# Layer one's narrow gate blocks as a pair of seven products, between two parts of the value pair

## The chip, the cores and the metric

The kernel runs on one core of one Trainium2 chip. The time is that of the device, in microseconds; the figure to be predicted is the median of several runs. A core has five engines that run their own instruction streams and meet at semaphores: TensorE (PE, matmuls; its weight loads are shown as PEld), VectorE (DVE), ScalarE (ACT), GpSimd (POOL) and SyncE (SP, which here issues most of the loads). DMA engines move data between the chip's memory and the on-chip buffers.

## The reference

A trunk of two layers over 512 tokens of 2048 features, in float32. Each layer normalises its input, projects it by one matrix whose columns serve two groups of heads and their gates, runs gated linear attention on one group and chunked attention on the other, and projects the result back:

```python
h = rmsnorm(x, g_pre)
z = h @ w_in
gq, gk, gv, gg, ga, aq, ak, av, ag = split_columns(z)
log_a = jax.nn.log_sigmoid((ga @ w_alpha + b_alpha).astype(jnp.float32)) / GLA_TAU
o_gla = gla_chunk_causal(...)
o_att = chunk_band_attention(...)
...
o_att = o_att * jax.nn.silu(ag)
y = jnp.concatenate([o_gla, o_att], axis=-1) @ w_out
return x + rmsnorm(y, g_post)
```

The change touches the columns `av` (values of the chunked attention, 1024 columns), `ag` (its gate, 1024) and `ga` (the 16 columns from which the forget gate is made). `ag` and `ga` are held as one block of 512 columns (AG0) and two narrow ones of 264 (AG1, AG2), the 16 of `ga` at the end of AG2.

## The kernel before, in words

**Products.** Each float32 operand is split into a high and a low part in PE's own format, and a product is the sum of three matmuls: high by high, high by low, low by high. The 2048 features are 8 chunks of 256; tokens are 4 groups of 128. Weights come as tiles of 128 x 1024 (two feature groups of 512 columns; 128 x 528 for a narrow block): a load by SP, a cast on ACT to the high part (`wh`, L240), a subtraction on DVE to the low part (`wl`, L250).

**Standard blocks and pairs.** `std_gemm` (L341) multiplies all tokens by one block: 8 chunk jobs of 24 matmuls. `fast_gemm` (L372) takes two blocks at once, as a 2 x 2 product of halves (tokens in two halves, features in two halves, two column blocks) with seven half-size products, P1 to P7, instead of eight. Each product has 4 chunk jobs (c0 to c3) of 12 matmuls. The price lies beside PE: sums and differences of weight tiles (L234, L236) and of token operands, and combinations of the accumulators at the end. The token sums are S1 to S4, the left operands of P5, P6, P3 and P7; P4's is A22, the second half of tokens and features. They are made in `make_sums` (L609), split, and written to memory by GpSimd; a later load brings them to a ring of four buffers, `sa`, which jobs use in turn.

**Order.** A list, `stream`, holds every job in the order in which PE takes them. `ahead()` (L295) prepares the jobs that follow: loads up to five jobs ahead, high parts four, low parts three. DVE work that does not belong to jobs (normalisation, sums, gates) is a list of `tasks`, advanced by `rate` steps a job; within an engine, instructions run in the order in which they were issued. Buffers in the ring and the named slots (`g0` to `g17`) can be taken again only when their last reader is done.

**The start of layer 0.** The wide block AG0 runs on raw tokens, since the normalisation is not known yet. Meanwhile `first_operands` (L706) normalises and splits the tokens, half after half within each chunk. Then the narrow blocks AG1 and AG2 run as standard blocks, while DVE makes the token sums. Then the value pair (AV0, AV1) runs all seven products in the order PROD; only S1 stays on the chip, the other sums are loaded. Then come the first query-key pair and the rest.

**Layer 1** already runs the narrow blocks as a pair (order PROD_GATE), and the value pair in two parts around half of AG0 (PROD_FRONT, PROD_REST).

Of the kernel before, what the change touches and what calls it, by code (L numbers as in the profile page):

```python
# [15 lines left out]
P = 128  # L16
# [20 lines left out]
def hybrid_trunk(  # L37
# [105 lines left out]
    PROD_REST = order("50 51 52 53 60 61 30 62 63 31 70 32 71 72 73 33 40 41 42 43")  # L143
    PROD_GATE = order("10 50 11 51 12 52 13 53 60 30 61 31 62 32 63 33 70 71 72 73 20 40 21 41 22 42 23 43")
# [6 lines left out]
    class Job:  # L151
        def __init__(self, l, kind, c, b0, b1=None, pair=None):
            self.l, self.kind, self.c, self.b0, self.b1, self.pair = l, kind, c, b0, b1, pair
            self.a = None
            self.parted = l == L - 1 and kind != "std" and b0 == AV0
# [19 lines left out]
        def load(self):  # L175
# [10 lines left out]
            elif k == "P1":  # L186
                h = slot(f"g{4 + c}", [2, 512]) if self.parted else rtile("H")
                p["H", self.c] = self.fetch(h, b0, top)
                last_h[0] = last_load[0]
            elif k == "P5" and self.parted:  # L190
# [3 lines left out]
            elif k == "P5":  # L194
                p["r", self.c] = self.fetch(rtile("raw", bufs=5), b1, top)
# [10 lines left out]
            else:  # L206
                home = k == "P5" and b0 == AV0
# [7 lines left out]
            elif src is not None and b0 != NB_IN and not home:  # L215
                until(lambda: k == "P4" or (id(sums), LEFT[k], c) in written)
# [7 lines left out]
        def high(self):  # L224
# [3 lines left out]
            else:  # L228
# [3 lines left out]
                with tc.issue_after(lows[-4 if early else -2]) if self.b0 >= NB_IN else nullcontext():  # L232
                    if k == "P6" or (k == "P5" and not self.parted) or (k == "P4" and (self.b0 >= NB_IN or self.parted)):
# [25 lines left out]
    for l in range(L):  # L259
        if l:  # L260
            pr = {}
            stream += [Job(l, "std", c, AG0) for c in CO]
            stream += [Job(l, k, c, *PAIRS[0], pr) for k, c in PROD_FRONT]
            stream += [Job(l, "std", c, AG0) for c in CO]
            stream += [Job(l, k, c, *PAIRS[0], pr) for k, c in PROD_REST]
            qk = {}
            pr = {"next": qk}
            stream += [Job(l, k, c, *GATE_PAIR, pr) for k, c in PROD_GATE]
        else:
            stream += [Job(l, "std", c, b) for b in (AG0, AG1, AG2) for c in CO]  # L270
        for b0, b1 in PAIRS[1:] if l else PAIRS:
            pr = qk if l and b0 == QK01 else {}
            stream += [Job(l, k, c, b0, b1, pr) for k, c in PROD]
# [28 lines left out]
    written = set()  # L302

# [36 lines left out]
    def std_gemm(l, blk, outs, chunks, operand, evac, rate=0.0, skip=0, lag=0):  # L340
        wide = W if blk == AG0 else N1  # L341
        pss = {o: ps_mm.tile([P, W], F32, tag="mm", name=nm("mm"))[:, :wide] for o in outs}
# [29 lines left out]
    def fast_gemm(l, pair, consume, rate=0.0, skip=0, feature_major=False, after=None, end=False, lag=0, ops=A, prod=None, acc=None):  # L372
        b0 = pair[0]
        gates = b0 == AG1
        wide = N1 if gates else W
        parted = acc is not None
        if not parted:
# [6 lines left out]
        if parted:  # L384
            target.update(P5="Z", P3="Z")
        if prod is None:
# [17 lines left out]
        def finished(k, t):  # L404
# [8 lines left out]
            elif k == "P2":  # L413
                consume(0, 0, t, None, combine(acc[target[k]][t], keep["p1"][t], ALU.add, keep["p1"][t]))
            elif k == "P4":
# [35 lines left out]
        for k, c in prod:  # L451
            if k == "P2" and (end or gates) and c == 0 or k == "P5" and parted and c == 0:
# [11 lines left out]
            with tc.issue_after(half_turns[1]) if (k, c) == ("P4", 3) and half_turns else nullcontext():  # L464
                matmuls(job, k, c, range(2))
            ahead()
# [44 lines left out]
    STAGE = ("g6", "g7", "g4", "g5", "g10")  # L511
    HOME = {("S1", c): tag for c, tag in enumerate(("g9", "g14", "g15", "g2"))}
    HOMES = {**HOME, **{("S2", c): tag for c, tag in enumerate(("g12", "g13", "g8", "g11"))}}
# [94 lines left out]
    def make_sums(dst, tags, parts, home={}):  # L608
        stage = [0]  # L609

        def sub(out, a, b):
            nc.vector.tensor_tensor(out=out, in0=a, in1=b, op=ALU.subtract)
# [13 lines left out]
        for c in range(4):  # L626
            a11, a12, a21, a22 = parts(c)
            yield
            sub(a22, a21, a22)
            put("S1", c, a22)  # L630
            yield
# [963 lines left out]
```

## Time and profile before

| what | value |
|---|---|
| median of 3 runs | 1590.28 us (1589.94 to 1592.12) |
| the profiled execution | 1594.45 us |
| its span in the profile | 1592.7 us |
| mean granted clock of PE | 0.999 |
| DMA | 441.45 MB, mean 277 GB/s |
| memory written | 61.62 MB |

The profile is of one execution, which took 1594.45 us; its span, from the first to the last instruction, is 1592.7. The costliest groups of instructions are matmuls of `fast_gemm` (L445; L435 where features are the rows of the result), then the casts and subtractions that split weights:

```profile
L445 PE MATMUL mm<-wh,sa 128*128 128x512 f32 (+1 forms) x1600 | 501.1, 387 | 1.8 <-DMA sa<-S 1.3
L240 ACT CAST wh<-H 128x1024 fp32r<-128x1024 f32 (+1 forms) x240 | 245.2, 1024 | 191.9 <-PE mm L445 78.9
L250 DVE TENSOR_TENSOR wl<-H,wh 128x1024 fp32r<-128x1024 f32 (+1 forms) x240 | 284.0, 1186 | 72.2 <-PE mm L445 25.4
```

Columns: line, engine, operation, output and inputs by the program's names, shapes and count; then the busy time in us and the mean of one in ns; then the idle time of the engine just before them, and what ended most of it. The mean of a matmul is longer than the time from one to the next, since matmuls overlap.

### The profile page before, as it was taken

The page shows a single profiled execution, that of the slowest core. Times are in us where ns is not written, and L with a number is a line of the kernel's source. Part 1 is how long each engine was busy: PE and PEld are TensorE (multiplying, and loading weights), DVE is VectorE, ACT ScalarE, POOL GpSimd, SP SyncE. Part 2 cuts the span into 40 slices and gives each one's busy share as a digit, 9 for nine tenths or more (in the row PEclk, how much of TensorE's full clock was granted, in tenths as well). Part 3 has the DMA queues.
Part 4 walks back from the last instruction along what each step waited for, and adds up shares of the span by engine and source line. Part 5 has one row for each costly group of instructions (what it writes and reads, how often), then busy time and mean ns, then how long its engine had stood idle before and what let it go on. Part 6 is the DMA issues. An engine that isn't in the chain of part 4 may idle for free.

```text
span 1592.7 us, 25038 instructions
## 1 busy us (share of the span) xinstructions
PE 1578.6 (99%) x9102; PEld 1369.3 (86%) x9102; DVE 1277.0 (80%) x1697; ACT 920.0 (58%) x1535; POOL 130.8 (8%) x222
## 2 busy tenths in 40 slices
PE   9999999999999999999999999999999999999998
PEld 7998999998888777888888899999988887778886
DVE  5978768678687878998989878775886878699887
ACT  7554445557465556664786456455574645476644
POOL 0220000000000000100122000000010000001001
PEclk9999999999999999999999999999999999999999
DMA  9698686685867869689889998847868597686887
GB/s 355 229 407 310 224 278 231 215 294 196 301 201 273 283 209 330 219 305 398 301 262 356 382 332 311 285 153 261 298 224 300 174 312 256 228 319 230 339 304 201
DMA packets 137739, 441.45 MB, mean 277 GB/s; under 512 B 15364, under 2 KB 27908, under 8 KB 137584
## 3 DMA queue, kind: packets, MB, share of 16 engines
q1 hardware_dynamic: 119952, 377.86, 67.5%
q0 software_dynamic: 17376, 61.70, 11.0%
q8 instruction: 72, 1.18, 0.3%
q14 instruction: 51, 0.42, 0.1%
q10 hardware_dynamic: 288, 0.30, 0.1%
HBM read 380.23 MB, written 61.62 MB: 277 GB/s over the span
## 4 chain that ended last, share of the span: by engine, by line
PE 86%; DVE 5%; DMA 5%; issue 2%; ACT 1%; SPq 0%; POOLq 0%; DVEq 0%; ACTq 0%
PE mm L445 51%; PE mm L435 17%; PE mm L358 6%; DMA raw<-in_w_dram 4%; PE ax L445 4%; DVE wl L250 2%; PE ax L1015 2%; PE ax L998 1%; PE ax L1204 1%; PE ax L1174 1%; PE ax L978 1%; PE ax L976 1%; PE ax L977 1%; ACT wh L240 1%; PE ax L1296 0%
## 5 line engine op out<-in xcount | busy, mean ns | idle before, releaser
L445 PE MATMUL mm<-wh,sa 128*128 128x512 f32 (+1 forms) x1600 | 501.1, 387 | 1.8 <-DMA sa<-S 1.3
L240 ACT CAST wh<-H 128x1024 fp32r<-128x1024 f32 (+1 forms) x240 | 245.2, 1024 | 191.9 <-PE mm L445 78.9
L445 PEld LDWEIGHTS mm<-wh,sa 128*128 128x128 f32 x1600 | 297.7, 188 | 64.9 <-ACT wh L240 3.0
L240 ACT CAST wh<-raw 128x1024 fp32r<-128x1024 f32 (+2 forms) x237 | 235.9, 1002 | 197.9 <-PE mm L445 87.4
L250 DVE TENSOR_TENSOR wl<-H,wh 128x1024 fp32r<-128x1024 f32 (+1 forms) x240 | 284.0, 1186 | 72.2 <-PE mm L445 25.4
L250 DVE TENSOR_TENSOR wl<-raw,wh 128x1024 fp32r<-128x1024 f32 (+2 forms) x237 | 272.5, 1154 | 49.3 <-PE mm L435 17.8
L445 PE MATMUL mm<-wl,sa 128*128 128x512 f32 (+1 forms) x800 | 310.1, 388 | 0.6 <-DVE wl L250 0.5
L435 PE MATMUL mm<-sa,wh 128*128 128x256 f32 x1280 | 237.8, 285 | 0.0
L445 PE MATMUL mm<-wh,a 128*128 128x512 f32 (+1 forms) x672 | 215.5, 387 | 0.0
L435 PEld LDWEIGHTS mm<-sa,wh 128*128 128x128 f32 x1280 | 200.3, 191 | 0.6
L435 PE MATMUL mm<-sa,wl 128*128 128x256 f32 x640 | 181.1, 284 | 0.5 <-DVE wl L250 0.5
L445 PEld LDWEIGHTS mm<-wl,sa 128*128 128x128 f32 x800 | 150.2, 188 | 31.9 <-DVE wl L250 2.3
L234 DVE TENSOR_TENSOR H<-H,raw 128x1024 f32<-128x1024 f32 (+1 forms) x136 | 160.8, 1185 | 1.6 <-DMA raw<-in_w_dram 1.0
L445 PEld LDWEIGHTS mm<-wh,a 128*128 128x128 f32 x672 | 125.2, 188 | 24.6
L445 PE MATMUL mm<-wl,a 128*128 128x512 f32 (+1 forms) x336 | 130.6, 389 | 0.5 <-DVE wl L250 0.5
L435 PEld LDWEIGHTS mm<-sa,wl 128*128 128x128 f32 x640 | 122.3, 191 | 0.9 <-DVE wl L250 0.9
L445 PE MATMUL mm<-wh,g 128*128 128x512 f32 (+1 forms) x416 | 120.4, 366 | 0.0
L236 DVE TENSOR_TENSOR raw<-H,raw 128x1024 f32<-128x1024 f32 (+1 forms) x52 | 61.5, 1182 | 48.4 <-DMA raw<-in_w_dram 48.3
L435 PE MATMUL mm<-a,wh 128*128 128x256 f32 x512 | 94.8, 285 | 0.0
L489 POOL TENSOR_TENSOR sm<-sm,mhalf 128x2 f32<-128x2 f32 (+2 forms) x40 | 38.0, 951 | 690.8 <-DVE sm L1025 367.1
L395 ACT COPY ev<-mm 128x512 f32<-128x512 f32 (+1 forms) x112 | 64.1, 573 | 52.8 <-PE mm L445 37.6
L445 PEld LDWEIGHTS mm<-wh,g 128*128 128x128 f32 x416 | 75.3, 188 | 13.4 <-ACT ev L395 0.6
(276 smaller groups left out, 2428.2 us busy)
## 6 DMA issues: line engine op xcount, KB each, us to landing
raw<-in_w_dram SPq DMA_DIRECT2D x287, 512.0 KB, 5.2
sa<-S SPq DMA_DIRECT2D x188, 512.0 KB, 4.7
H<-in_w_dram SPq DMA_DIRECT2D x56, 512.0 KB, 5.1
sa<-A SPq DMA_DIRECT2D x48, 512.0 KB, 6.3
sa<-oS SPq DMA_DIRECT2D x32, 512.0 KB, 5.7
S<-g POOLq DMA_DIRECT2D x30, 512.0 KB, 8.1
raw<-in_w_ag_dram SPq DMA_DIRECT2D x32, 264.0 KB, 4.3
oS<-g POOLq DMA_DIRECT2D x16, 512.0 KB, 4.8
```

Of the source, the lines that this page charges most:

```text
L234: nc.vector.tensor_tensor(out=h, in0=h, in1=r, op=ALU.add)
L236: nc.vector.tensor_tensor(out=r, in0=h, in1=r, op=ALU.subtract)
L240: last_cast[0] = nc.scalar.copy(self.wh[:, z, :], src[:, z, :]).ins
L250: last_low[0] = nc.vector.tensor_tensor(out=self.wl[:, z, :], in0=self.src[:, z, :], in1=self.wh[:, z, :].bitcast(F32), op=ALU.subtract).ins
L358: nc.tensor.matmul(pss[o], a(part, kk, o) if callable(a) else a[:, part, t], rhs[:, kk, :], start=(i == 0 and kk == 0 and m == 0), stop=(i ...
L395: last_copy[0] = nc.scalar.copy(e, src[t]).ins
L435: nc.tensor.matmul(dst, lhs[:, kk, f], a[:, part, tok], start=(fresh and kk == 0 and m == 0 and ft % 2 == 0), stop=(c == 3 and kk == 1 and ...
L445: last_mm[0] = nc.tensor.matmul(out_ps[t], a[:, part, tok], rhs[:, kk, :], start=(fresh and kk == 0 and m == 0), stop=(c == 3 and kk == 1 ...
L489: nc.gpsimd.tensor_tensor(out=out_r, in0=v, in1=mhalf[:, : v.shape[-1]], op=ALU.pow)
L976: nc.tensor.matmul(ps[:, :n], self.qh[:, t], self.kh[:, :n], start=True, stop=False)
L977: nc.tensor.matmul(ps[:, :n], self.qh[:, t], self.kl[:, :n], start=False, stop=False)
L1015: nc.tensor.matmul(o, self.pt[i][:, j * P : (j + 1) * P], av[hd // 4, j // 2][:, j % 2, (hd % 4) * P : (hd % 4 + 1) * P], start=(j == 0), ...
```

## The change

In layer 0 the narrow blocks become a pair of seven products, and the order of work becomes: AG0 whole; P2 and P1 of the value pair; P2 and P1 of the narrow pair; P5, P6, P3, P7, P4 of the value pair; the same five of the narrow pair. The accumulators of the narrow pair's first products stay in the auxiliary PSUM buffers in the meantime. The tokens are normalised by halves: the first half of all chunks, then the second. The sums are made name by name (S1, S2, S4, S3) instead of chunk by chunk, S3 after P3 has been issued; they stay on the chip for the value pair, which therefore loads only A22. For the narrow pair S4, S3, A22 and the last chunk of S1 are loaded. P5's weight sum in the value pair is made by an accumulating DMA of GpSimd onto the tile of P1, no longer by DVE; the narrow pair's P1 tile is loaded a second time for P5. The first operands of the first query-key pair are loaded into slots early, as layer 1 does already. Layer 1's own orders are as they were.

The core of the diff:

```diff
+    PROD_LATE = order("50 51 52 53 60 61 62 63 30 31 32 33 70 71 72 73 40 41 42 43")
+    PROD_LATE_GATE = order("50 51 52 53 60 61 62 63 30 31 70 32 71 33 72 73 40 41 42 43")
...
-            self.parted = l == L - 1 and kind != "std" and b0 == AV0
+            self.parted = kind != "std" and (b0 == AV0 or (b0 == AG1 and l == 0))
+            self.summed = self.parted and b0 == AV0
...
-                h = slot(f"g{4 + c}", [2, 512]) if self.parted else rtile("H")
+                h = slot(f"g{4 + c}", [2, 512]) if self.summed else rtile("raw", bufs=5) if self.parted else rtile("H")
...
             elif k == "P5":
+                if self.parted:
+                    p["H", self.c] = self.fetch(rtile("H"), b0, top)
                 p["r", self.c] = self.fetch(rtile("raw", bufs=5), b1, top)
...
-                home = k == "P5" and b0 == AV0
+                home = b0 == AV0 and k != "P4" or b0 == AG1 and (k == "P6" or (k == "P5" and c < 3))
...
+        pr, qk = {}, {}
+        pg = {"next": qk}
+        stream += [Job(l, "std", c, AG0) for c in CO]
+        stream += [Job(l, k, c, *PAIRS[0], pr) for k, c in PROD_FRONT]
         if l:
...
         else:
-            stream += [Job(l, "std", c, b) for b in (AG0, AG1, AG2) for c in CO]
+            stream += [Job(l, k, c, *GATE_PAIR, pg) for k, c in PROD_FRONT]
+            stream += [Job(l, k, c, *PAIRS[0], pr) for k, c in PROD_LATE]
+            stream += [Job(l, k, c, *GATE_PAIR, pg) for k, c in PROD_LATE_GATE]
...
+            elif l == 0:
+                op = A[name, c] = rtile("sa", (2, 512), F32R)
...
+            for name in ("S1", "S2", "S4", "S3"):
+                for c in range(4):
+                    while name == "S3" and (0, AV0, "P3", c) not in issued:
+                        yield
+                    make(name, c)
+                    yield
...
-        for ch in CO:
-            kh, c = divmod(ch, 4)
-            while ch not in U:
-                yield
-            for half in range(2):
+        for half in range(2):
+            for ch in CO:
+                kh, c = divmod(ch, 4)
+                while ch not in U:
+                    yield
...
+                if half and kh == 0:
+                    ends.append(made.ins)
+                    yield
+                    continue
...
-            tasks.append(token_sums(l))
-            std_gemm(l, AG1, range(NT), CO, operand_in, gate_evac(1), rate=1.0, lag=1)
-            std_gemm(l, AG2, range(NT), CO, operand_in, gate_evac(2), rate=1.0, lag=2)
-            drain()
...
-            fast_gemm(l, PAIRS[0], av_consume, rate=0.5)
+            std_gemm(l, AG0, range(NT), CO, operand_raw, raw_evac, rate=0.25, lag=1)
+            acc = {n: [ps_mm.tile([P, W], F32, tag="mm", name=nm("mm")) for _ in range(2)] for n in "YX"}
+            fast_gemm(l, PAIRS[0], av_consume, rate=2, prod=PROD_FRONT, acc=acc)
+            acc_g = {n: [aux()[:, :N1] for _ in range(2)] for n in "YX"}
+            tasks.append(token_sums(l))
+            fast_gemm(l, GATE_PAIR, gate_consume, rate=1, prod=PROD_FRONT, acc=acc_g)
+            acc["Z"] = [ps_mm.tile([P, W], F32, tag="mm", name=nm("mm")) for _ in range(2)]
+            fast_gemm(l, PAIRS[0], av_consume, rate=1, prod=PROD_LATE, acc=acc)
+            drain()
+            fast_gemm(l, GATE_PAIR, gate_consume, prod=PROD_LATE_GATE, acc=acc_g)
```

Counted over the whole program: PE has 720 matmuls of 264 columns before and 672 after, with all others alike; DVE goes from 1697 to 1727 instructions, ACT gains 12 casts of 528 columns and 8 copies of 264 among others, SP's DMAs go from 777 to 790 and POOL's from 158 to 162.

Two places of the instruction order. The first is DVE where the value pair's second weight sums begin. Before, the weight lows (`wl`) and the weight sums of P6 (into `H`) of the value pair stand almost alone:

```order
L250 TENSOR_TENSOR wl_199_1287<-H_190_1184,wh_192_1212 128x1024
L250 TENSOR_TENSOR wl_200_1289<-H_187_1154,wh_198_1285 128x1024
L234 TENSOR_TENSOR H_190_1184<-H_190_1184,raw_203_1295 128x1024
L800 COPY g16_195_1231<-mm_173_1025 128x16 x3
L250 TENSOR_TENSOR wl_209_1320<-H_201_1291,wh_202_1293 128x1024
L250 TENSOR_TENSOR wl_212_1339<-H_190_1184,wh_210_1323 128x1024
L234 TENSOR_TENSOR H_201_1291<-H_201_1291,raw_214_1343 128x1024
```

In the changed kernel the same engine, where the value pair goes from P5 to P6 (`g4` to `g6` hold the weight tiles; L630 makes a token sum and L110 its low part; `wl_191_1067` is the low part for P6, chunk 0):

```order
L630 TENSOR_TENSOR H_89_512<-H_89_512,g2_127_718 128x512
L241 TENSOR_TENSOR g4_107_632<-g4_107_632,raw_181_1014 128x1024
L110 TENSOR_TENSOR g8_178_994<-g2_127_718,g8_178_994 128x512
L257 TENSOR_TENSOR wl_187_1043<-g7_126_716,wh_180_1012 128x1024
L241 TENSOR_TENSOR g5_116_662<-g5_116_662,raw_189_1048 128x1024
L630 TENSOR_TENSOR H_100_589<-H_100_589,g3_134_749 128x512
L110 TENSOR_TENSOR g11_184_1025<-g3_134_749,g11_184_1025 128x512
L241 TENSOR_TENSOR g6_121_689<-g6_121_689,raw_193_1072 128x1024
L243 TENSOR_TENSOR raw_212_1193<-g4_107_632,raw_212_1193 128x1024
L257 TENSOR_TENSOR wl_191_1067<-g4_107_632,wh_188_1046 128x1024
```

Token sums and their lows now stand between the weight work, ahead of P6's first low part; before, they were done in the narrow blocks.

The second place is SP, where the operand A22 of the value pair's P4 is loaded (`A2200` is chunk 0 in memory). Before, sums and weight tiles take turns:

```order
L172 DMA raw_274_1660<-in_w_dram 128x1024
L219 DMA sa_264_1602<-S302_92 128x1024
L172 DMA raw_281_1701<-in_w_dram 128x1024
L219 DMA sa_268_1623<-S303_93 128x1024
L172 DMA raw_288_1741<-in_w_dram 128x1024
L219 DMA sa_277_1679<-A2200_98 128x1024
L172 DMA raw_303_1832<-in_w_dram 128x1024
L219 DMA sa_284_1719<-A2201_99 128x1024
```

In the changed kernel at the same operand (`g14`, `g15`, `g2` are the first operands of the next pair, `in_w_ag` is the narrow blocks' weights):

```order
L175 DMA raw_225_1264<-in_w_dram 128x1024
L175 DMA raw_229_1288<-in_w_dram 128x1024
L175 DMA g14_286_1562<-in_w_dram 128x1024
L175 DMA raw_235_1317<-in_w_dram 128x1024
L175 DMA g15_292_1586<-in_w_dram 128x1024
L175 DMA raw_239_1338<-in_w_dram 128x1024
L175 DMA raw_243_1359<-in_w_dram 128x1024
L175 DMA g2_300_1627<-in_w_dram 128x1024
L226 DMA sa_231_1295<-A2200_98 128x1024
L167 DMA raw_248_1382<-in_w_ag_dram 128x528
L167 DMA raw_256_1412<-in_w_ag_dram 128x528
L226 DMA sa_236_1319<-A2201_99 128x1024
```

The loads of S3 are gone; three tiles of the next pair stand in front of A22 instead, and the weight tiles follow one another without an operand between.

More of the change, by code (lines that the diff above doesn't have):

```diff
@@ L215, in load @@
             elif src is not None and b0 != NB_IN and not home:
+                if self.summed and not self.l:
+                    until(lambda: ("S3", 3) in A)
                 until(lambda: k == "P4" or (id(sums), LEFT[k], c) in written)
@@ L302, in hybrid_trunk @@
     written = set()
+    issued = set()
     def pump(n):
@@ L340, in std_gemm @@
     def std_gemm(l, blk, outs, chunks, operand, evac, rate=0.0, skip=0, lag=0):
-        wide = W if blk == AG0 else N1
-        pss = {o: ps_mm.tile([P, W], F32, tag="mm", name=nm("mm"))[:, :wide] for o in outs}
+        pss = {o: ps_mm.tile([P, W], F32, tag="mm", name=nm("mm")) for o in outs}
         pace = Pace(rate, skip)
@@ L373, in fast_gemm @@
         b0 = pair[0]
-        gates = b0 == AG1
-        wide = N1 if gates else W
         parted = acc is not None
+        apart4 = parted and not l
+        gates = b0 == AG1 and not parted
+        wide = N1 if b0 == AG1 else W
         if not parted:
@@ L385, in fast_gemm @@
             target.update(P5="Z", P3="Z")
+        if apart4:
+            target.update(P4="Z")
+            starts.append("P4")
         if prod is None:
@@ L451, in fast_gemm @@
         for k, c in prod:
-            if k == "P2" and (end or gates) and c == 0 or k == "P5" and parted and c == 0:
+            if k == "P2" and (end or gates) and c == 0 or k == "P5" and parted and c == 0 and "Z" not in acc:
                 acc["Z"] = [aux()[:, :wide], aux()[:, :wide]]
@@ L731, in first_operands @@
                 ends.append(split(op[:, 0, :], op[:, 1, :], dst))
-                if half and kh:
+                if half:
                     nc.gpsimd.dma_start(sa_d[0]["A22", c], flat(op))
@@ L735, in first_operands @@
                 yield
-        yield from load_forget_gate(0)
     warm = t2((S,), BF16)
@@ L763, in load_forget_gate @@
     def load_forget_gate(l):
-        raw = slot("g10" if l else "g12", [2, 512])
+        raw = slot("g10", [2, 512])
         fac = slot("g13", [2, 512], F32R)
@@ L894, in raw_evac @@
             gate(0, o, ps, r0[:, o : o + 1])
[L896 to L903 removed]
         av = {}
[L906 removed]
+        AVT = {1: ("g0", "g1"), 0: ("g17", "g3")}
         def av_consume(j, h, t, src, comb):
             if (j, h) not in av:
[L910 removed]
+                if not l:
+                    until(lambda: all((1, 1, c) in A for c in range(4)))
+                av[j, h] = slot(AVT[j][h], [2, 512])
             dst = av[j, h][:, t, :]
```

90 lines of the change are left out of this document (44 added, 46 removed).

## The prediction

> **What bounds the kernel now.** The page's busy shares come first, then the chain that ended last.
>
> ```profile
> PE 1578.6 (99%) x9102; PEld 1369.3 (86%) x9102; DVE 1277.0 (80%) x1697; ACT 920.0 (58%) x1535; POOL 130.8 (8%) x222
> PE 86%; DVE 5%; DMA 5%; issue 2%; ACT 1%; SPq 0%; POOLq 0%; DVEq 0%; ACTq 0%
> ```
>
> TensorE (PE) is the bound, but 99% flatters it: matmul ends are modelled, so a short wait can hide in "busy". I therefore count matmuls. Two rows of the chain in layer 1, where twelve matmuls of one product and chunk run together, give the pitch:
>
> ```profile
> 883.40 2.72 PE mm L445 x12
> 954.01 1.44 PE mm L445 x12
> ```
>
> These are 2.72 / 12 = 0.227 us for a matmul of 512 columns and 1.44 / 12 = 0.120 us for one of 264. Next I cut the start of layer 0 into stretches (columns after the span's length: PE, PEld, DVE, ACT, POOL busy with instructions; then granted clock, DMA share, GB/s):
>
> ```profile
> 36.00:56.00 20.00, 20.00 (x110) 17.43 (x109) 20.00 (x40) 12.54 (x21) 3.66 (x7) 1.00 0.54 181
> 56.00:76.00 20.00, 19.03 (x150) 18.15 (x149) 19.98 (x38) 12.56 (x24) 3.69 (x8) 1.00 0.80 262
> 76.00:100.00 24.00, 24.00 (x197) 23.83 (x196) 20.73 (x39) 12.96 (x23) 9.75 (x19) 1.00 1.02 388
> 100.00:174.00 74.00, 74.00 (x329) 61.07 (x328) 56.04 (x55) 33.38 (x37) 1.67 (x3) 1.00 0.90 335
> ```
>
> The clock is full throughout. From 36 to 76 us VectorE (DVE) is busy without a gap; from 56 to 76 only 150 narrow matmuls ran, 150 x 0.120 = 18.0 us of work in 20: **2.0 us were lost**. The chain names the engine:
>
> ```profile
> 34.63 21.42 PE mm L358 x114
> 56.05 0.62 DVE wl L250
> 56.67 0.60 DVE g L612
> 58.40 0.88 DVE H L719 x2
> 59.29 0.60 DVE g L110
> ...
> 75.15 24.79 PE mm L358 x200
> ```
>
> Weight lows (L250), gate work (L612), first normalisation (L719) and operand lows (L110) were taken one after another on DVE, and PE waited. After 76 us PE runs unbroken. So layer 0's narrow blocks start DVE-bound and end PE-bound.
>
> **The change part by part.**
>
> 1. *Fewer matmuls.* The two narrow blocks go from 384 matmuls to 7 x 4 x 12 = 336, all of 264 columns; no other count changes. 48 x 0.120 = **-5.8 us**, if PE stays the bound.
>
> 2. *The old DVE stall goes* with the blocks that had it: after the wide block PE now has value products of 2.72 us a chunk, each needing one weight low, where a narrow one lasted 24 x 0.120 = 2.88 us and needed a low and an operand. **-2.0 us** (0 to -2.0).
>
> 3. *What is late next.* DVE's work isn't gone: the sums for the value pair must now be made before its late products begin. In the changed order the place is P6, chunk 0, of the value pair. For the DVE durations:
>
> ```profile
> 36.38 0.87 DVE L719 SCALAR_TENSOR_TENSOR H<-g,gcol,bias 128x256 f32<-128x256 f32 x2
> 37.17 0.87 DVE L719 SCALAR_TENSOR_TENSOR g<-g,gcol,bias 128x256 f32<-128x256 f32 x2
> 37.96 2.73 DVE L119 SCALAR_TENSOR_TENSOR g<-g,gcol,sa 128x512 fp32r<-128x512 f32 x4
> 40.61 0.68 DVE L110 TENSOR_TENSOR a<-H,a 128x512 fp32r<-128x512 f32 x1
> ...
> 107.84 1.22 DVE L234 TENSOR_TENSOR H<-H,raw 128x1024 f32<-128x1024 f32 x1
> 108.97 0.68 DVE L815 COPY g<-ax 96x512 f32<-96x512 f32 x1
> ```
>
> From start to start: 0.79 us for a pair of L719, so 0.40 each; 2.65 for four of L119; 1.13 for 1024 columns. From the first normalisation to the low of P6 c0, the changed order has 38 operations of 512 columns (20 operand or sum lows, 16 sums, 2 gate steps) at 0.60 = 22.8; 8 narrow lows at 0.62 = 5.0; 18 of 1024 columns (14 lows, 4 weight sums) at 1.13 to 1.14 = 20.4; 32 normalisation halves at 0.40 = 12.8; 4 of L119 = 2.65; and 2 combinations of 264 columns, which no row shows, about 0.35 each by half the 0.62 of 528. In all 64.35 us without a gap, begun at 36.38 as now (nothing ahead of it moves): the low ends at 100.7. PE's side:
>
> ```profile
> 50.80 0.28 PE L358 MATMUL mm<-wh,a 128*128 128x264 f32 x1
> ```
>
> The wide block ends at 50.80. Then 8 value jobs, 8 narrow jobs and P5's 4 value jobs: 8 x 2.72 + 8 x 1.44 + 4 x 2.72 = 44.2, so P6 c0 can start at 95.0; its first two matmuls need only the high half, 0.45 more. 100.7 - 95.4 = 5.3 of waiting, and 0.2 at the next chunk: **+5.5 us**. Start-to-start durations hold to about 1.5%, which is 1 us in 64: 4.5 to 6.5. I take the middle. It is a difference of two long sums, and so the term I trust least.
>
> 4. *The A22 operand of P4, chunk 0* (value pair). Its load takes the ring buffer that P7 c0 sets free; P4 c0 starts 3 products later, 3 x 2.72 = 8.2 us. The lead is the same now, and nothing waits, as these rows show:
>
> ```profile
> L219 SPq DMA_DIRECT2D sa<-A x48: 319/382/1386, 146.8 to 1406.7; - x48
> DMA to landing us min/median/max: 3.3/6.5/11.3
> ```
>
> In the changed order nine SP loads (six weight tiles of products and three first operands of the next pair, taken ahead of time) stand between the tile of P7 c0 and this operand, and three POOL stores beside them: 12 x 0.524 = 6.3 MB within the 13.6 us of five products. That is 463 GB/s asked. What the engines gave when full, between 85 and 120 us:
>
> ```profile
> DMA packets 4077, 14.34 MB, mean 410 GB/s; under 512 B 524, under 2 KB 524, under 8 KB 4072
> q1 hardware_dynamic: 2247, 7.97, 56.0%
> q0 software_dynamic: 1825, 6.31, 46.0%
> raw<-in_w_dram SPq DMA_DIRECT2D x9, 512.0 KB, 13.9
> ```
>
> So a backlog forms: 6.3 MB at 410 GB/s take 15.3 us, 1.7 over. The landing lies between 6.5 (median of this operand) and 13.9 us (a load of the same size in the full stretch): a wait between 0 and 13.9 - 8.2 = 5.7. Neither end is nearer: demand is above what they gave, as in the full stretch, but for a short time only. I take 10.5: **+2.3 us**.
>
> [...]
>
> 5. *The rest of the narrow pair* is 20 jobs of 12 matmuls, 28.8 us. DVE's share: 16 weight sums or differences and 20 lows at 0.62, and 8 combinations at 0.35 to 0.7: 25 to 28 us. It is nearly a second bound. Layer 1 runs such a pair today:
>
> ```profile
> 924.00:948.00 24.00, 24.00 (x192) 23.62 (x191) 18.23 (x28) 13.51 (x26) 0.00 (x0) 1.00 0.86 297
> ```
>
> 192 x 0.120 = 23.0 in 24: 1.0 lost. For 28.8 us that is **+1.2 us** (0.3, if DVE's work spreads evenly, to 2.4, twice the row, as DVE is fuller here).
>
> 6. *The first query-key pair* finds its first four operands loaded. It loses today:
>
> ```profile
> 220.00:232.00 12.00, 11.49 (x94) 11.17 (x94) 7.59 (x8) 4.03 (x4) 0.00 (x0) 1.00 0.73 257
> 212.58 5.42 DMA raw<-in_w_dram
> 220.49 6.50 DMA raw<-in_w_dram
> ```
>
> 0.5 idle, and the chain goes through its loads: **-0.3 us** (0 to -0.9).
>
> 7. *Costed at nothing.* Twelve more casts of 528 columns and eight copies on ScalarE (ACT): ACT is busy 12.96 of 24 us and 33.38 of 74. Uncovered they would be 20 x about 0.5 = 10 us, but they lie over 120 us of PE work. Four weight loads of P5 become accumulating DMAs of POOL, which the order issues over 20 us ahead of P5:
>
> ```profile
> g<-in_w_dram POOLq DMA_DIRECT2D x4, 512.0 KB, 7.6
> ```
>
> 7.6 us to landing in layer 1, so they are hidden; if the lead went, each would cost up to 7.6 - 2.72 = 4.9. The new wait of S3's four sums for P3 keeps those sums behind P3's operands on DVE; behind them stand the lows of P7 and P4, two products ahead of PE. DVE is busy 56.04 of 74 there, so I cost it at nothing; without that slack it would be S3's own 12 operations, 7.2 us, spread over P3 and P7.
>
> **Sum:** -5.8 - 2.0 + 5.5 + 2.3 + 1.2 - 0.3 = **+0.9 us**. The profiled execution took 1594.45 (span 1592.7); with the change 1595.35 (span 1593.6). It lies 4.2 above the median of the runs, 1590.28, so the forecast for the median is **1591.2 us**. The matmuls saved are eaten by a DVE wait that has moved and grown, and by a load that comes late.
>
> **The rivals.**
>
> *A, slower: the DMA backlog decides.* Term 4 at its upper end: A22 lands 13.9 us after its issue, 5.7 late, and the total is 0.9 - 2.3 + 5.7 = +4.3, **1594.6 us**. The place is the wait ahead of P4 c0 of the value pair, the point 8.2 us from issue to landing. For it: 463 GB/s asked where 410 was the most seen, and POOL's stores in the same engines. Against it: the engines are 0.90 busy, not full, over the 74 us of the present value pair, and the DVE wait of term 3 gives the loads 5.5 us to catch up.
>
> *B, faster: DVE keeps up.* If the 64 us of DVE work come out 3.5 shorter (the normalisation halves at 0.29, say) and A22 is in time: -5.8 - 2.0 + 2.0 + 0 + 1.2 - 0.3 = -4.9, **1585.4 us**. For it: many of these operations had waits of others between them in the row I took them from. Against it: DVE shows 20.00 and 19.98 busy of 20 in two stretches with this very mix.
>
> *C: the change doesn't do what it says.* The late narrow pair is DVE-bound from end to end, so 48 fewer matmuls buy nothing there: term 5 at 2.4 and one more microsecond for the four combinations that fall together at P7: +3.1, **1593.4 us**. For it: 28 of 28.8 us. Against it: layer 1's row, DVE 18.23 of 24.
>
> **How the numbers follow.** Forecast 0.60, A 0.20, B 0.13, C 0.07. The forecast's own range is -2 to +3, from term 3 (1 either way) and term 4 (2.3 down). For 8 in 10 it must reach into A and most of the way to B: **1586.5 to 1595.8**. About 0.2%, 3.2 us, is what a measurement of this kernel can tell from no change: below 1587.1 lies B with little else, 0.14; above 1593.5 lie A and the upper part of C, 0.23; between them 0.63.
>
> **What would show it.** Right: the first narrow stretch (after the wide block) shows no PE idle; one wait of 4.5 to 6.5 us on DVE (a weight low) about 95 us, at the start of P6; then one of 1 to 4 us on a DMA of an A22 operand about 130 to 140; 336 narrow matmuls in layer 0; from the query-key pair on, the same times with a constant offset. Term 3 is wrong if DVE has gaps between 40 and 95 us or PE's wait there is under 3; term 4 if the operand lands within 8.2; term 5 if the last 240 narrow matmuls take under 29.1 or over 31.2 us. The whole is wrong if layer 1 shifts against layer 0, which nothing in the instruction order suggests.

## The result

The layer that the title calls one is layer 0 of the code. The changed kernel takes 1604.09 us (median; 1603.16 to 1604.71), the kernel before 1590.47 in the same series (1589.94 to 1592.12): 13.6 us slower, a ratio of 1.0083 with a 95% interval of 1.0066 to 1.0101. The forecast was 1591.2 with a range of 1586.5 to 1595.8, so it is wrong: a time above 1593.5 had been given a chance of 0.23, and even the upper rival, 1594.6, is 9.5 us short.

The page of the changed kernel (busy shares, and the chain that ended last by engine):

```profile
PE 1575.7 (98%) x9054; PEld 1365.9 (85%) x9054; DVE 1291.4 (81%) x1727; ACT 927.2 (58%) x1551; POOL 135.4 (8%) x226
PE 86%; issue 4%; DMA 4%; DVE 3%; ACT 1%; POOL 1%; SPq 0%; POOLq 0%; DVEq 0%; ACTq 0%
```

48 matmuls are gone, and the span is 1601.9 us instead of 1592.7. The stretches of layer 0's start (columns as before, granted clock after the busy times):

```profile
36.00:56.00 20.00, 19.15 (x85) 15.50 (x84) 20.00 (x40) 14.24 (x21) 2.42 (x4) 1.00 0.80 293
56.00:76.00 20.00, 20.00 (x99) 16.96 (x98) 19.79 (x31) 9.69 (x16) 5.74 (x8) 1.00 0.87 214
76.00:100.00 24.00, 20.22 (x118) 18.24 (x118) 20.68 (x30) 13.08 (x22) 4.83 (x9) 0.93 0.92 361
100.00:140.00 40.00, 35.54 (x154) 28.27 (x152) 34.44 (x36) 21.01 (x27) 4.79 (x9) 1.00 0.79 285
140.00:174.00 34.00, 31.19 (x196) 28.36 (x197) 23.38 (x35) 12.63 (x23) 0.78 (x2) 0.95 0.94 338
```

The old loss between 56 and 76 us is gone. In its place PE idles 3.8 us in the third row, 4.5 in the fourth and 2.8 in the fifth, and the granted clock, 1.00 everywhere before, is 0.93 and 0.95 in two of them. The waits of PE from 40 to 200 us (engine and line, what it waited for: us in total, times, longest):

```profile
PE mm L459 <- DMA sa<-A: 3.6, 1, 3.6
PE mm L459 <- DVE wl L257: 2.7, 2, 1.7
PE mm L459 <- ACT wh L247: 2.6, 1, 2.6
PE ax L459 <- ACT wh L247: 1.2, 1, 1.2
PE ax L459 <- DMA sa<-S: 1.1, 1, 1.1
PE ax L459 <- DVE wl L257: 0.9, 2, 0.5
PE mm L366 <- DVE wl L257: 0.9, 1, 0.9
```

13.0 us, against 0.9 before. Three groups matter: 3.8 us on casts at 82 to 87 us, 1.7 on the low part of P6 at 102, and 3.6 on the A22 operand at 138.

**How much of it lies there.** The last 8000 matmuls are the same in both kernels. The matmul with 8000 behind it starts, counted in the traces, at 196.6 us before (196.4 in a second profile) and at 207.0 now: 10.4 to 10.6 us later. From it to the last matmul it is 1390.6 and 1388.2 us in the two profiles of before, 1389.9 in the changed one. So the change's loss lies ahead of this point; the rest moves by 2.4 us between two profiles of one kernel. That the medians differ by 13.6 and the start by 10.5 is partly this; I could not place the last 2 to 3 us.

**The first group, followed back.** ACT's instructions in order of time (start, duration, operation; in brackets the idle time before and what ended it):

```profile
83.02 0.63 ACT L247 CAST wh<-raw 128x528 fp32r<-128x528 f32 x1 [4.05 <-DMA raw<-in_w_ag_dram]
83.56 0.61 ACT L109 CAST g<-g 128x512 fp32r<-128x512 f32 x1
84.08 0.37 ACT L407 COPY ev<-ax 128x264 f32<-128x264 f32 x1
84.35 0.63 ACT L247 CAST wh<-raw 128x528 fp32r<-128x528 f32 x1
84.88 0.38 ACT L407 COPY ev<-ax 128x264 f32<-128x264 f32 x1
85.15 0.63 ACT L109 CAST g<-g 128x512 fp32r<-128x512 f32 x1
85.67 1.05 ACT L247 CAST wh<-g 128x1024 fp32r<-128x1024 f32 x1
```

The cast is not the cause. ACT stood still for 4 us for a narrow weight tile, and then worked off what had queued behind it; the last row is the cast for the value pair's P5, for which PE waits until 86.8. The vector engine stood still with it, for 3.3 us, since the low part of a token sum needs ACT's cast of the high part:

```profile
84.20 0.69 DVE L110 TENSOR_TENSOR g<-g,g 128x512 fp32r<-128x512 f32 x1 [3.29 <-ACT g L109]
```

From there it works without a gap up to P6's first low part, and PE goes on at P6 when that is done:

```profile
104.31 0.50 PE L459 MATMUL mm<-wl,g 128*128 128x512 f32 x1 [1.70 <-DVE wl L257]
```

Why the tile was late shows in the DMA queues between 62 and 78 us (q0: GpSimd's; q1: SP's; packets, MB, share of 16 engines; then issues with the median time to landing):

```profile
q0 software_dynamic: 924, 3.40, 92.2%
q1 hardware_dynamic: 257, 0.48, 8.5%
...
g<-in_w_dram POOLq DMA_DIRECT2D x3, 512.0 KB, 8.5
raw<-in_w_ag_dram SPq DMA_DIRECT2D x3, 264.0 KB, 8.5
```

GpSimd's queue, with four accumulating loads and four stores of A22, holds the engines for 92% of 16 us; SP's narrow tiles take 8.5 us.

**The clock.** In the two stretches behind the two long waits:

```profile
87.00:91.00 4.00, 4.00 (x20) 3.90 (x20) 4.00 (x7) 2.76 (x4) 0.95 (x2) 0.57 1.01 408
...
142.00:145.00 3.00, 3.00 (x7) 2.36 (x8) 1.88 (x4) 0.00 (x0) 0.00 (x0) 0.50 1.03 413
```

PE runs at about half its clock for 3 to 4 us, and loses 4 x 0.43 = 1.7 and 3 x 0.50 = 1.5 us more. The first of the two does not lengthen the whole: without it PE would only have waited longer for P6's low part, as e5 shows.

**The A22 operand**, by the chain of waits:

```profile
124.07 6.45 DMA S<-sa
...
130.58 11.21 DMA sa<-A
...
141.92 3.32 PE mm L459 x7
```

The load starts when the store of S3, chunk 0, has left the ring buffer, and takes 11.2 us.

### The profile page after: what moved, and what is told of

The parts are those of the page before. It is cut to its first block, busy times and chain, and to the rows that moved or that the text cites. A ratio compares the mean times of both kernels' runs of the same rounds, so it can differ in the third digit from the quotient of the medians.

```text
span 1601.9 us, 25047 instructions
## 1 busy us (share of the span) xinstructions
PE 1575.7 (98%) x9054; PEld 1365.9 (85%) x9054; DVE 1291.4 (81%) x1727; ACT 927.2 (58%) x1551; POOL 135.4 (8%) x226
## 3 DMA queue, kind: packets, MB, share of 16 engines
q0 software_dynamic: 17952, 63.79, 11.5%
## 4 chain that ended last, share of the span: by engine, by line
PE 86%; issue 4%; DMA 4%; DVE 3%; ACT 1%; POOL 1%; SPq 0%; POOLq 0%; DVEq 0%; ACTq 0%
PE mm L459 49%; PE mm L449 20%; PE ax L459 5%; PE mm L366 4%; PE ax L1049 2%; DMA sa<-A 1%; DMA raw<-in_w_dram 1%; DVE wl L257 1%; PE ax L1032 1%; PE ax L1238 1%; PE ax L1208 1%; DMA sa<-S 1%; PE ax L1012 1%; PE ax L1011 1%; PE ax L1010 1%
## 5 line engine op out<-in xcount | busy, mean ns | idle before, releaser
L459 PE MATMUL mm<-wh,sa 128*128 128x512 f32 (+1 forms) x1568 | 492.2, 388 | 5.7 <-DMA sa<-A 4.9
L459 PEld LDWEIGHTS mm<-wh,sa 128*128 128x128 f32 x1568 | 292.8, 188 | 67.9 <-ACT wh L247 5.4
L247 ACT CAST wh<-H 128x1024 fp32r<-128x1024 f32 (+1 forms) x220 | 219.5, 999 | 182.0 <-PE mm L459 75.5
L459 PE MATMUL mm<-wl,sa 128*128 128x512 f32 (+1 forms) x784 | 304.6, 389 | 4.3 <-DVE wl L257 4.3
L257 DVE TENSOR_TENSOR wl<-H,wh 128x1024 fp32r<-128x1024 f32 (+1 forms) x220 | 254.3, 1157 | 62.8 <-PE mm L459 27.1
L241 DVE TENSOR_TENSOR H<-H,raw 128x1024 f32<-128x1024 f32 (+1 forms) x132 | 149.9, 1140 | 1.2 <-DMA raw<-in_w_ag_dram 0.8
L459 PE MATMUL mm<-wh,g 128*128 128x512 f32 (+1 forms) x448 | 129.9, 368 | 2.6 <-ACT wh L247 2.6
L247 ACT CAST wh<-g 128x1024 fp32r<-128x1024 f32 x68 | 71.0, 1054 | 61.8 <-DVE g L241 23.2
L257 DVE TENSOR_TENSOR wl<-g,wh 128x1024 fp32r<-128x1024 f32 x68 | 82.8, 1223 | 22.6 <-PE mm L449 11.6
L459 PEld LDWEIGHTS mm<-wh,g 128*128 128x128 f32 x448 | 81.3, 188 | 17.3 <-ACT wh L247 3.3
```

Source lines behind the costliest of these rows:

```text
L241: nc.vector.tensor_tensor(out=h, in0=h, in1=r, op=ALU.add)
L247: last_cast[0] = nc.scalar.copy(self.wh[:, z, :], src[:, z, :]).ins
L257: last_low[0] = nc.vector.tensor_tensor(out=self.wl[:, z, :], in0=self.src[:, z, :], in1=self.wh[:, z, :].bitcast(F32), op=ALU.subtract).ins
L459: last_mm[0] = nc.tensor.matmul(out_ps[t], a[:, part, tok], rhs[:, kk, :], start=(fresh and kk == 0 and m == 0), stop=(c == 3 and kk == 1 ...
```

## The experiments

All but e0 are edits of the changed kernel, or of an earlier experiment where said. The kernel before ran beside each of them: 1591.16 us beside e1 to e3, 1590.89 beside e4 to e7, 1590.86 beside e8 and e9, 1590.89 beside e10 and e11.

**e0, the kernel before once more.**

> The kernel before, profiled a second time. The first value product of the query-key pair starts at 176.5 us of the first profile, 185.5 in the changed kernel's. If the 13.6 us of the medians come from layer 0's changed start alone, this start stays at 176.5 within 0.3; what else differs between two profiles of the same kernel is chance in how loads fall, and must not be read as the change's.

Its first query-key product starts at 176.3 us (176.5 in the first profile), its span is 1590.5 instead of 1592.7. It gave the second profile of the count above.

**e1, A22 in slots of its own, the next pair's operands in the ring.**

```diff
-            if b0 == AG1 and k == "P3":
+            if b0 == AG1 and k == "P3" and self.l:
...
-                self.a = rtile("sa", (2, 512), F32R)
+                if self.summed and not self.l and k == "P4" and c < 3:
+                    self.a = slot(("g14", "g15", "g2")[c], [2, 512], F32R)
+                else:
+                    self.a = rtile("sa", (2, 512), F32R)
```

> The changed kernel, but the A22 operands of the value pair's P4, chunks 0 to 2, get slots of their own (those of the next pair's early operands, which are loaded later, into the H ring, as before the change). Theory (the load is late because its ring buffer comes free only when the store of S3 chunk 0 has landed at 130.5 us): the load is issued near 124, lands by 134, the wait of 3.8 us at 138 and the half-clock stretch of 1.5 us behind it go, and the whole is 5 us faster, less up to 0.9 for the next pair's operands. Rival (the engines are full there, whoever issues): the load still lands near 141, and the time stays within 1 us.

1607.14 us, 3 slower than the changed kernel instead of 4 to 5 faster. The wait on A22 is gone, and so is the wait of 1.2 ahead of it. But the query-key pair now loses 8.3 us between 180 and 200 (starts of matmuls, less the pitch). ACT there:

```profile
183.47 1.04 ACT L250 CAST wh<-H 128x1024 fp32r<-128x1024 f32 x1
190.58 1.04 ACT L250 CAST wh<-H 128x1024 fp32r<-128x1024 f32 x1 [6.07 <-DMA H<-in_w_dram]
```

The operand loads are issued from 173 us on, when the narrow pair frees its tiles, and come late. Theory confirmed for A22; and the early load of these operands, which I had valued at 0.3 us, is worth some 8 in this order.

**e2, the stores of A22 later.**

```diff
                 if half:
-                    nc.gpsimd.dma_start(sa_d[0]["A22", c], flat(op))
+                    unstored.append((c, op))
...
                 for c in range(4):
+                    if (name, c) == ("S1", 2):
+                        for i, op in unstored:
+                            nc.gpsimd.dma_start(sa_d[0]["A22", i], flat(op))
```

> The changed kernel, but the four stores of A22 (2.1 MB) are issued after the narrow pair's last front weights, near 80 us, in place of 61 to 73. Theory (these stores and the accumulating loads fill the engines, so that the narrow weights land 8.3 us after their issue and PE waits 4.1 us at 82 to 87): the narrow weights land within 6 us, the wait falls below 2 us and the half clock behind it goes; then the vector engine's wait at P6 chunk 0, 1.9 us now, takes its place at 4 to 5.5 us, so that only 2 to 4 us are gained in all. Rival (the loads are late for being issued late, since the vector engine frees their buffers): the wait of 4.1 us stays within 1 us and the time within 1 us.

1602.48 us. This one tells nothing: the stores still leave at 62 to 74 us, since the program's scheduler puts what is ready back to the front. It counts as a second run of the changed kernel.

**e3, P5's weight sum on the vector engine.**

```diff
-            elif k == "P5" and self.summed:
+            elif k == "P5" and self.summed and self.l:
...
-                    if k == "P6" or (k == "P5" and not self.summed) or (k == "P4" and (self.b0 >= NB_IN or self.parted)):
+                    if k == "P6" or (k == "P5" and not (self.summed and self.l)) or (k == "P4" and (self.b0 >= NB_IN or self.parted)):
```

> The changed kernel, but P5's weight sum of the value pair is made on the vector engine from a plain load, as before the change: four accumulating loads go from GpSimd's queue, four vector operations of 1.14 us come ahead of P6. Theory (the accumulating loads hold the engines: 232 GB/s at a full share between 66 and 72 us): the stretch 66 to 72 shows a higher rate or a smaller share, the wait at 82 to 87 shrinks by 2 us or more, and P6's wait on the vector engine grows by about 4.6 plus what is won earlier; the whole within 2 us of the changed kernel. Rival (accumulating costs the engines no more than a plain load): the rate at a full share is as low, the wait at 82 to 87 stays, and the whole is 3 to 5 us slower.

1604.55 us, no different. The same stretch of the DMA queues, 62 to 78 us:

```profile
q0 software_dynamic: 576, 2.10, 34.6%
q1 hardware_dynamic: 795, 1.47, 28.6%
...
raw<-in_w_ag_dram SPq DMA_DIRECT2D x3, 264.0 KB, 3.0
```

The narrow tiles land after 3.0 us instead of 8.5, and the waits on casts are gone. In their place stands the vector engine:

```profile
PE mm L459 <- DVE wl L257: 6.2, 2, 5.4
```

The long wait is at P5, whose weight sums are now on the vector engine; the expectation had put it at P6, where 0.8 us are lost:

```profile
91.79 0.80 PE L459 MATMUL mm<-wl,g 128*128 128x512 f32 x1 [5.37 <-DVE wl L257]
```

The accumulating loads do make the tiles late; taking them away uncovers 5.4 us of vector work.

**e4, the stores of A22 pinned behind a later store.** As e2, with

```diff
-            nc.gpsimd.dma_start(dst[name, c], flat(op))
+            last_store[0] = nc.gpsimd.dma_start(dst[name, c], flat(op)).ins
...
+                        with tc.issue_after(last_store[0]):
+                            for i, op in unstored:
+                                nc.gpsimd.dma_start(sa_d[0]["A22", i], flat(op))
```

> The changed kernel, but the four A22 stores are pinned behind the store of S1 chunk 1, so that they leave near 80 us (in e2 the scheduler had put them back to 62 to 74). Theory (accumulating loads and these stores together hold the engines while the narrow weights wait): without the stores the narrow weights land about 2 us sooner (8.3 to 8.6 us after the issue now, 2.6 to 3.4 in e3 without accumulating loads), the two waits of 1.4 and 2.7 us at 82 to 87 fall to 2 us or less together, no half clock follows them, and the vector engine's wait at P6 grows to 4 or more; 1 to 4 us faster in all. Rival (the accumulating loads alone do it): the landings stay above 7.5 us, and the time within 1 us.

1598.55 us, 5.5 faster, where 1 to 4 were expected. Now 62 to 78 us holds only the four accumulating loads in GpSimd's queue:

```profile
q0 software_dynamic: 576, 2.10, 72.6%
...
raw<-in_w_ag_dram SPq DMA_DIRECT2D x3, 264.0 KB, 4.4
```

The waits on casts are gone. The wait on the vector engine at P6 has grown, as the theory had it, from 1.7 to 3.1 us, and the granted clock behind it is 0.58:

```profile
100.88 0.78 PE L459 MATMUL mm<-wl,g 128*128 128x512 f32 x1 [3.07 <-DVE wl L257]
...
101.00:105.00 4.00, 4.00 (x11) 3.19 (x12) 4.00 (x5) 1.56 (x2) 0.93 (x2) 0.58 0.75 259
```

By the count used above, only 1.5 us of the 5.5 lie in the start of layer 0: the matmul with 8000 behind it starts at 205.5 instead of 207.0, for part of what is won goes again in the half clock behind P6 and in a wait of 2.0 us on a stored sum at 172, with a granted clock of 0.93 over 152 to 176 us. The other 4 us are not placed.

**e5, e1 with the next pair's operands loaded ahead.** Only the second half of e1's edit, so that the operands follow A22 into the same slots.

> The changed kernel with A22 chunks 0 to 2 of the value pair in slots of their own, as in e1, but with the next pair's operands loaded ahead into the same slots after P4 has read them. Theory: as in e1 no wait at 138 and no half clock behind it (-5.3), the vector wait of 1.2 at 134 gone too, and the query-key pair without e1's 8.3 us of loss: 5 to 6.5 us faster than the changed kernel. Rival (the loss of e1 at the query-key pair came from crowded engines, not from late issue): 2 us or more of it stay at 180 to 200, and the gain is 1 to 4 us.

1599.08 us, 5.0 faster, and the count agrees (202.4 instead of 207.0). Nothing is lost from 120 to 140 us, and nothing at the query-key pair. In this profile the granted clock behind the wait of 2.6 us on a cast at 87 us is 1.00 (87 to 91), and yet P6 goes on no sooner than in the changed kernel; its wait is longer instead:

```profile
104.38 0.50 PE L462 MATMUL mm<-wl,g 128*128 128x512 f32 x1 [3.18 <-DVE wl L260]
```

So the vector engine sets the time of P6. And A22's wait was a matter of its buffer, and e1's loss one of late issue.

**e6, eight low parts on GpSimd.**

```diff
+                if l == 0 and name in ("S1", "S2"):
+                    nc.scalar.copy(op[:, 0, :], src)
+                    nc.gpsimd.tensor_tensor(out=op[:, 1, :], in0=src, in1=op[:, 0, :].bitcast(F32), op=ALU.subtract)
+                else:
+                    split(op[:, 0, :], op[:, 1, :], src)
```

> The changed kernel, but the eight low parts of S1 and S2 are made by GpSimd, which takes 8 x 0.60 = 4.8 us off the vector engine ahead of P6. Theory (the vector engine is the bound of the stretch 40 to 105 us, and by freeing weight buffers late it also causes late loads): the waits at 82 to 87 shrink by 1 to 2, P6's wait of 1.9 goes, and the whole is 3 to 5 us faster. Rival (the full DMA engines set the waits at 82 to 87, whatever the vector engine does): those 4.1 us stay, only P6's wait goes, 2 us faster. Second rival: GpSimd takes 2 us or more for one, and delays its own stores and loads: no gain.

1602.46 us: no gain is shown, since e2, the changed kernel once more, took 1602.48, and the matmul with 8000 behind it starts at 206.9 instead of 207.0. This is the second rival, but for a reason I had not named. The eight operations on GpSimd (75 to 96 us holds seven), and the narrow lows of the vector engine between 75 and 90 us (mean in ns after the busy time; a mean of 703 for the same five without the change):

```profile
L644 POOL TENSOR_TENSOR g<-g,g 128x512 fp32r<-128x512 f32 x7 | 10.0, 1430 | 7.1 <-ACT g L643 7.0
L257 DVE TENSOR_TENSOR wl<-raw,wh 128x528 fp32r<-128x528 f32 x5 | 6.8, 1383 | 1.6 <-ACT wh L247 1.6
```

Beside subtractions on GpSimd a vector operation took up to 1.9 us here, instead of 0.7. The work taken off one engine came back as waiting.

**e7, e4, e5 and e6 together.**

> The changed kernel with e4, e5 and e6 together. If the causes are separate: the waits of layer 0 fall from 20 to 8 us or less, 10 to 12 us faster than the changed kernel, within 2 us of the kernel before. If each removed wait uncovers the next (the vector engine), 5 to 8 us faster.

1603.05 us, neither of the two: no gain beyond the 1.6 us by which e2 differs from the changed kernel. The eight subtractions on GpSimd take 3.04 us each in the mean here: seven between 74 and 96 us take 10.7 in all, which leaves some 13.6 for the eighth. PE waits 1.7 us for one of them.

**e8, e4 and e5 without e6.**

> The changed kernel with e4's held stores and e5's slots, vector work where it was. If the two causes are separate, e4's P6 wait on the vector engine stays (3 to 4 us with 1 to 1.6 of half clock behind it), e5's empty stretch from 120 to 140 stays, and layer 0's lost time falls from 20 us to 11 to 13; 6 to 8 us faster than the changed kernel. If GpSimd's additions were not what spoiled e7, this one shows 2 us or more of new waits on the vector engine at 80 to 92, as e7 did.

1593.96 us, 10.1 faster than the changed kernel, where 6 to 8 were expected (8.8 by the count, 198.2 instead of 207.0); a ratio of 1.0017 (1.0008 to 1.0027) to the kernel before. Against e7 it has the eight low parts back on the vector engine, and is 9 us faster. The largest waits left:

```profile
PE mm L462 <- DVE wl L260: 3.5, 2, 3.1
PE ax L462 <- DMA sa<-S: 1.5, 2, 1.3
```

**e9, e8 with another order of vector work.**

```diff
+                    while name == "S4" and (0, AV0, "P5", 1) not in issued:
+                        yield
...
-                sub(a12, a12, a22, ALU.add)
+                with tc.issue_after(last_low[0]) if not l else nullcontext():
+                    sub(a12, a12, a22, ALU.add)
...
-                with tc.issue_after(lows[-4 if early else -2]) if self.b0 >= NB_IN else nullcontext():
+                with tc.issue_after(lows[-4 if early else -2]) if self.b0 >= NB_IN or self.summed and not self.l and k != "P5" else nullcontext():
```

> e8, and the vector engine's order is changed ahead of P6: S4's four sums (2.4 us), the weight sum of P6 chunk 2 and the weight difference of P7 chunk 0 (2.3 us) stand behind P6 chunk 0's low part instead of ahead of it. Nothing is computed otherwise. Theory (P6's wait is 64 us of vector work against 59 of PE): 4.7 us off that sum takes the wait at 97 from about 3.3 to under 1, with no half clock behind it; 4 to 5 us faster than e8, within 3 us of the kernel before. Rival (the work moved behind is late at P3 instead): a wait of 2 us or more on an operand or a low part appears at 106 to 120, and at most 2 us are gained.

1591.42 us, not to be told from the kernel before (ratio 1.0002, 0.9993 to 1.0012), and 2.5 faster than e8, where 4 to 5 were expected. The wait at P6 is gone. The stretch 80 to 104 us in the changed kernel, in e8 and in e9:

```profile
80.00:104.00 24.00, 18.84 (x95) 16.08 (x93) 20.71 (x28) 14.69 (x23) 4.83 (x9) 0.93 0.81 323
```

```profile
80.00:104.00 24.00, 20.50 (x105) 17.00 (x105) 24.00 (x32) 15.25 (x23) 7.36 (x14) 0.96 0.99 374
```

```profile
80.00:104.00 24.00, 23.81 (x125) 20.15 (x124) 24.00 (x32) 17.02 (x26) 7.46 (x14) 1.00 0.99 378
```

95, 105 and 125 matmuls, while the vector engine is busy 20.7, 24.0 and 24.0 of 24 us. It is full in both e8 and e9; what e9 changes is only which of its work comes first. No wait came up at P3. New waits of 3.3 us in all, on casts, appear at 146 to 165 and take part of the gain back.

**e10, e9 with A22 kept for the narrow pair.**

```diff
+                p["a22", c] = kept.get((self.l, c))
+                if p["a22", c] is None:
+                    p["a22", c] = slot(f"g{4 + c}", [2, 512], F32R)
+                    nc.sync.dma_start(flat(p["a22", c]), sums["A22", c])
...
-                    self.a = slot(("g14", "g15", "g2")[c], [2, 512], F32R)
+                    self.a = kept[0, c] = slot(("g14", "g15", "g2")[c], [2, 512], F32R)
```

> e9, but the narrow pair's P4 uses the A22 operands, chunks 0 to 2, that the value pair's P4 has loaded, in place of loading them again (1.6 MB less between 130 and 140 us, where the engines run full at 411 GB/s), and the next pair's first operands go to the slots that this leaves free. Theory (the waits of 1.2 to 3.2 us at 146 to 151 are loads that stand behind one another in full engines): those waits fall by half or more, 1 to 3 us faster than e9, so 589 to 590 against 591 for the kernel before, counted from 1000: 1588.5 to 1590.5. Rival (they are the order of casts on the scalar engine): they stay within 0.5 us and so does the time.

1590.28 us (ratio 0.9999, 0.999 to 1.0008). The waits on casts are gone, 2.0 us on stored sums and 1.2 on low parts have come; layer 0's start is 2 us shorter (the matmul with 8000 behind it at 193.5 instead of 195.5), which the medians don't separate from nothing. That start is also 3 us ahead of the kernel before, whose median is only 0.6 higher: here, too, some 2 us behind it are not placed.

**e11, e10 with the normalisations behind the wide block's lows.**

```diff
-                with tc.issue_after(ends[-2]) if len(ends) >= 2 else nullcontext():
+                with tc.issue_after(ends[-2]) if len(ends) >= 2 else nullcontext(), \
+                     tc.issue_after(last_low[0]) if half == 0 else nullcontext():
```

> e10, and the first half's normalisations are pinned behind the weight lows of the wide block. Theory (the wait of 1.0 to 1.3 us at 46 is a weight low that stands behind normalisations and operand lows in the vector engine's queue): that wait goes; the work held back comes later, so that 0.5 to 1.2 us of it return as a wait on a low part at 85 to 100; 0 to 1 us faster than e10.

1588.95 us (ratio 0.9994, 0.9984 to 1.0003). The wait at 46 us is gone and 1.0 us on a low part has come at 85, as expected. The median is the lowest of all, but the start is 1 us later than e10's (194.6), so that the gain does not come from there, and the interval holds 1: no version is shown to beat the kernel before.

## Why the prediction was wrong

Times in this section are of the profiles: lost time is what the starts of matmuls show beyond the pitch.

1. *48 fewer matmuls*: right. 9054 matmuls in place of 9102, and every kernel here has the saving.
2. *The old vector stall goes*: right; nothing is lost from 56 to 76 us. A smaller one, 1.0 us at 46, came instead: normalising the first half of all chunks puts normalisations and operand lows ahead of a weight low of the wide block. That was not in the sum; e11 shows it.
3. *Vector work ahead of P6*: the sum was right, its place in the time was not. The low part was forecast to end at 100.7; in e4, where hardly anything waits ahead of it, PE goes on at 100.88. In the changed kernel it goes on at 104.3, since the vector engine itself had stood still for 3.3 us with the casts. What PE waited for there was 1.7 us, because PE had been stopped earlier for something else: the 5.5 us were paid, but under other names.
4. *A22*: right in kind, wrong in size and half of the reason. I took 10.5 us to landing and 8.2 of lead; it was 11.2 and 7.5, for the lead was cut by the store of S3, which holds the buffer longer than P7 does and which I had left out. 3.6 us idle, plus the half clock. e5 shows the buffer as the cause.
5. *The late narrow pair*: 1.2 forecast; 0.9 us on low parts and 1.1 on stored sums idle. The sums' loads were not in the term.
6. *The query-key pair*: -0.3 forecast. The changed kernel loses nothing there; the two profiles of before lose 0.9 and nothing. e1 shows what the early load covers in the new order: 8.3 us.
7. ***Costed at nothing* is the step that failed.** Of the accumulating loads I wrote that they take 7.6 us to landing and are issued over 20 us ahead, "so they are hidden". They are: the last lands at 79, and the first cast for P5 comes at 81.3 even in e4, where nothing delays it. What I did not price is what they do to others. Four of them held the engines for 72.6% of 16 us (e4), with the four stores 92.2%, and in that time the narrow weights of P1, loaded only when a buffer came free at 69 to 75 us (at the same times in e3 and e4), landed 5.5 us later than in e3. That put P6 off by 3.4 us, the largest single miss, though no one step makes up the whole. The cover that I checked was their own; the load beside them had none.
8. *The clock*: I read 1.00 in every stretch of before and did not ask what a longer wait would do. The half clock behind A22's wait cost 1.5 us on top of it; the 1.7 behind the cast wait vanished in the wait at P6.

By size: the start of layer 0 was forecast 1.2 us longer (the sum without term 6) and is 10.5 longer. P6 goes on 3.4 us after the forecast 100.7 to 100.9, for the vector engine's standstill; the wait at 46 and the first half clock are not added to this, since they lie ahead of P6, whose time the vector engine sets. Behind P6, A22 took 1.4 more than the term and its half clock 1.5; a wait of 1.2 on a low part at 134 was in no term; the late narrow pair took 1.7 more (2.9 lost in all). Together these are 9.2. The old loss that went was 2.6, not 2.0 (2.2 between 60 and 80 us and 0.4 later), which leaves 8.6 against a difference of 9.3; the last 0.7 is not placed.

Rival A had the right side and one of the places, with a wait of 5.7 us where 3.6 were measured; it had neither the clock nor the loads at 62 to 78, so that it came nearest is in part luck. Rival B needed a vector engine that keeps up; e9 shows that this needs another order, not less work. What e8 and e9 together give back, 12.7 us of the 13.6 in the medians and 11.5 in the start (195.5 instead of 207.0), shows the causes as named: stores beside accumulating loads, the ring buffer of A22, and the order ahead of P6. Their shares do not add up one by one: in the start e4 alone wins 1.5 us, e5 alone 4.6, both together 8.8.

## What to carry to other kernels

A transfer that lands in time can still be the cause of a wait: here the accumulating loads were in time, while the narrow weights, beside them and four stores, took 8.5 us to landing, and 3.0 in e3 without accumulating loads. Ask of each added transfer not only when it is needed but whose loads go through the engines beside it, and when the buffers of those come free. Where one engine is full for a long stretch, as the vector engine is for 24.0 of 24 us in e8 and e9, removing one wait can uncover the next (5.4 us in e3), and the order within the full engine decided here (e9) more than what was moved off it (e6). And since behind eight of ten waits of 2.4 to 5.4 us the granted clock was below full here, a prediction that has PE wait so long should price the clock behind it, and ask whether a later wait hides that price.

## What the runs showed of the hardware

**The accumulating loads of e4 held the DMA engines for 11.6 us, as many MB of stores in e3 for 5.5.** Between 62 and 78 us GpSimd's queue moved 2.10 MB in e4, all accumulating, in 72.6% of 16 us, 11.6 us; in e3 2.10 MB of plain stores in 34.6%, 5.5 us. SP's plain loads in e3 took 28.6% for 1.47 MB, 4.6 us: per MB that is 5.5 us for accumulating loads, 2.6 for stores and 3.1 for plain loads, in these two runs.

**Behind eight of ten waits of 2.4 us or more the granted clock was below full.** The ten are waits of PE between 80 and 145 us behind which stretches of the granted clock lie, in the changed kernel, e2 to e5 and e8. The clock was below 1.00 behind 2.6 and 3.6 us in the changed kernel (0.57 over 87 to 91 us, 0.50 over 142 to 145), 3.1 in e2 (0.93 over 80 to 104), 5.4 in e3 (0.50 over 91 to 95), 3.1 and 2.4 in e4 (0.58 over 101 to 105, 0.68 over 137 to 141), 3.2 in e5 (0.93 over 104 to 128) and 3.1 in e8 (0.66 over 101 to 105). It was 1.00 behind 2.6 in e5 (87 to 91) and 3.3 in e3 (137 to 145). In the changed kernel the clock was at 0.50 from 87.31 to 90.73 us and from 141.93 to 145.34, 3.41 us each time, for 1.7 and 1.5 us of lost work; its changes lie 3.41, 51.20 and 3.41 us apart, 1, 15 and 1 times 3.41. The length of the wait does not tell the cases apart: at the same operand, A22, e3 waited 3.3 us and kept the clock, e4 waited 2.4 and did not. No stretch here shows what does. The rows of e3 and then of e4 (columns as before):

```profile
137.00:141.00 4.00, 1.27 (x6) 0.73 (x4) 3.65 (x4) 3.06 (x4) 0.00 (x0) 1.00 1.02 417
141.00:145.00 4.00, 3.43 (x15) 2.88 (x16) 2.65 (x5) 0.35 (x1) 0.00 (x0) 1.00 1.05 419
```

```profile
137.00:141.00 4.00, 3.64 (x11) 2.91 (x12) 2.38 (x4) 0.00 (x0) 0.00 (x0) 0.68 1.04 416
141.00:145.00 4.00, 3.90 (x17) 3.02 (x15) 2.30 (x3) 0.90 (x2) 0.00 (x0) 0.89 1.03 407
```

**Vector operations took longer beside subtractions on GpSimd.** In e6, with seven subtractions of 1.43 us on GpSimd, the mean of five narrow lows was 1383 ns, against 703 in the changed kernel, and one vector operation took up to 1.9 us instead of 0.7. What the eight subtractions cost on GpSimd is seen in e7 and e8, which differ in this work alone, and by 9 us; part of that is waits for GpSimd's own results, 1.7 us for one of them.
